# Sooner Pool forms, a three-step last map, group 0's first z tile moved, and another place for the third gate block

## The chip, the cores and the metric

The kernel runs on one core of one Trainium2 chip. The metric is the device time of one execution in microseconds (us). A core has engines that run side by side, each through its own list of instructions in order, and wait for one another by semaphores: PE (TensorE, the matmuls), ACT (ScalarE), DVE (VectorE), POOL (GpSimd) and SP (SyncE). SP, POOL and ACT also issue DMA transfers, each in the order of its own list.

## The reference

One layer of a hybrid trunk for 384 tokens (256 of a new stream, 8 times 16 of running ones), d_model 2048, in float32. One wide projection gives the columns for pool, z, x/B/C, dt and gates. Branch A is a causal pooling with a map for each of four channel groups; branch B is a Mamba-2 scan in eight groups; two gated projections are added, then an MLP follows.

```python
def pool_mixer(p, st, pos0, pool_w, pool_scale):
    ...
    for g, w in enumerate(POOL_WINDOWS):
        ...
        d = win / cnt[None, :, None] - p[:, :, lo:hi].astype(jnp.float32)
        outs.append(jnp.einsum('blc,cd->bld', d.astype(p.dtype), pool_w[g]))
    out = jnp.concatenate(outs, axis=-1) * pool_scale
    ...
        cb = jnp.einsum('btgn,bsgn->btsg', Cc, Bc)
        xdt = xc * dtc[..., None]
        y = jnp.einsum('btsgr,bsgrp->btgrp', cb[..., None] * decay, xdt)
        y = y + jnp.einsum('btgn,bgrpn->btgrp', Cc, h) * jnp.exp(cum)[..., None]
    ...
    br_pool = (a_pool @ p['w_pool_proj']).astype(jnp.float32)
    br_ssd = (a_ssd @ p['w_ssd_proj']).astype(jnp.float32)
    merged = (gates[:, :, 0] * br_pool + gates[:, :, 1] * br_ssd).astype(u.dtype)
    out = merged @ p['w_out']
```

## The kernel before

Weights come in units of 128 x 1024 floats, half a MB, that SP loads (`wfetch`, L64). Every float32 product is made of three: ACT copies a unit to a high half (`wh_...`, L71), DVE subtracts it for the low half (`wl_...`, L72), and PE multiplies high by high (L102), high by low (L103) and low by high (L104). A projected tile of 128 channels by 384 tokens uses two units, 24 matmuls each. `take` keeps up to three split units ahead, so that ACT makes one split for each 24 matmuls of PE, between other work. Both the loads on SP and the splits on ACT and DVE follow a queue of units that is written out (L988 on). A tile of a projection goes to one of two PSUM buffers (`mmtile`); what empties it runs on DVE.

PE's own order is forced: each `half` is issued behind the last matmul of the one before. A helper `behind(ins)` issues a piece after another, and `later()` puts it behind the newest weight split on ACT and on DVE. For the rest a scheduler sets each engine's order.

The Pool branch. Sixteen tiles p0 to p15 are projected, four for each of the maps 0 to 3 (`pool_tile`, L455 on: DVE empties the PSUM tile, L468 to L470, and ACT keeps the last rows, L478). `pool_map(gi)` multiplies the windowed tiles by the map's weights ("pw"), and ACT writes the scaled result to the tile px (L535). What follows is put on a list, `steps`: a `tick()` after each weight unit takes one entry of each list. The entries are five differences on DVE (`diff`), and five pieces, each a copy on ACT (L546), a subtraction on DVE (L547) and a store to DRAM (L548), from px to pf. Map 0 has four empty entries ahead of these. px and pf are single buffers, so that map 1 writes them only when map 0's pieces and stores are through. `dt_turn` (L615 on) turns the dt columns by 11 small PE transposes ("tk", L627) and copies them to `tok` on DVE (L628, L635); it stands behind tile (2, 1), which is p9.

The scan. Group 0 has its x, B, x, C, x, x tiles and four z tiles projected, in this order in the queue. A `conv_in` moves a tile to a cbuf with the last rows of the state; `taps` makes the convolution: a first tap on ACT (L678), three more on DVE (L680), a silu on ACT (L684, with a load of the activation table where another function ran before). `t_cb` multiplies C by B (cb, L753), `t_yi` multiplies the state hs by C (py, L762); then x's next tile is projected. Group 0's convolutions belong to the pool `phd`, whose first instruction comes behind the last of `phc`, with the pieces of map 3. `eside` (L894) and `expside` (L903) form the decay E on ACT. x is turned to tokens through DRAM (t_scr, L708 to L720, on POOL), and state comes by POOL too (hs, L741).

The end of the mixer's first half. Three blocks of the gate of branch A are stored to ga_scr for later (`stored`); the blocks 1 and 2 use the ring "hs" of the scan's pool for their output ("gat"). Block 2 (ga2, 24 matmuls for each of its eight weights) runs beside the end of the scan. Then the matrix products of w_pp and w_ssd begin, by a scheme of seven products from quarter blocks ("sq", L1229 to L1231). `load` (L1183 on) fetches four blocks b12, b11, b21, b22 on SP, and POOL adds b11's source to b12 by an accumulating DMA (L1189): that is U. W, V and b22 follow from it by sums on DVE (L1216). Slots of the left operand are read back from p_scr by `refill` (as, ab, aU, aW, aV, aX; L1303). "as" of the second block of rows is read at step 6 of the first.

The lines that touch all this in the code before:

Of the kernel before, what the change touches and what calls it, by code (L numbers as in the profile page):

```python
# [14 lines left out]
P = 128  # L15
# [18 lines left out]
def build(ctx, tc, io):  # L34
# [234 lines left out]
    def in_units(i):  # L269
        return [win[i - 5, 0], win[i - 5, 1]]  # L270
# [177 lines left out]
    with tc.tile_pool(name="phc", bufs=1, reuse_waits="tile") as pc, tc.tile_pool(name="phc2", bufs=2, reuse_waits="tile") as pc2:  # L448
# [73 lines left out]
        def pool_map(gi, after=None):  # L522
            for hf in range(2):
                h, l = wload(io["pool_w"][gi, hf], f"pw{gi}_{hf}")
                for n2 in range(2):
                    n = gi * 4 + hf * 2 + n2
                    o = sstile(f"pw{n}")[:, :T]
                    with behind(after):
                        for k in range(4):
                            c = slice((n2 * 4 + k) * P, (n2 * 4 + k + 1) * P)  # L530
                            mm3w(o, h[:, c], l[:, c], dd[gi][k][0], dd[gi][k][1], k == 0, k == 3)
                    if hf + n2 == 0:
                        x = pc.tile([P, 2, 10, P], F32, tag="px", name=f"px{gi}")
                    a = x[:, n2, hf * 3 : hf * 3 + 3].rearrange("p s t -> p (s t)")
# [14 lines left out]

            wait = [lambda: None] * (0 if gi else 4)  # L550
            steps.append(wait + [diff] + [lambda i=i: piece(i) for i in range(5)])

# [102 lines left out]
        for gi in range(4):  # L655
            for k4 in range(4):
# [9 lines left out]
                if gi == 1 and k4 > 1:  # L666
                    with later():
                        next(dt_steps, None)
                if (gi, k4) == (2, 1):
                    dt_turn()  # L670
# [3 lines left out]
    with tc.tile_pool(name="phd", bufs=2, reuse_waits="tile") as pd:  # L674
# [313 lines left out]
        for g in range(G):  # L988
            cs = [g * 4, 32 + g, g * 4 + 1, 40 + g, g * 4 + 2, g * 4 + 3]
            names = [f"x{c}" for c in cs] + [f"z{g}_{j}" for j in range(4)]  # L990
            queue.extend((in_units(17 + g * 10 + i)[q], f"{nm}_{q}") for i, nm in enumerate(names) for q in range(2))
        queue[:4] = []
        queue.extend(u for nb in (1, 2) for u in units_of("w_ga", nb))
        prev = None
        for g in range(G + 1):
            if g == G:
# [37 lines left out]

                stored("w_ga", 2, [mmtile("ga2_0"), sstile("ga2_1"), sstile("ga2_2")], gtiles(2), closing)
                break
# [40 lines left out]
            cside(D)  # L1077
            b2 = conv_in(u0 + 4, g * 4 + 2)
            S = D.p[0]
            S.py = mmtile(f"py{S.nm}")  # L1080
# [21 lines left out]

            def zproj(j):
                ps = proj(in_units(u0 + 6 + j), xg, f"z{g}_{j}")
                z = pd.tile([P, T], F32, tag="zs", name=f"zs{g}_{j}", bufs=8)
                with later():
                    v.tensor_tensor(halves(z), even_odd(ps), halves(rstd), ALU.mult)
                    s.activation(z, z, AF.Silu)
                D.zs.append(z)

            zproj(0)
            if g:
# [219 lines left out]
    def group(gk, np_):  # L1332
# [4 lines left out]
        def extra(i):  # L1337
# [25 lines left out]
            if gk < 3:  # L1363
                if t == 6:
                    refill(gk + 1, "s2")
                if t > 6:
                    refill(gk + 1, ORDER[t - 7])
                return
# [699 lines left out]
```

## Time and profile before

| | us |
|---|---|
| median of 3 runs | 2601.79 (2601.68 to 2604.74) |
| the profiled execution | 2603.8 |
| its span on the core | 2602.0 |
| PE busy in it | 2568.6 |
| ACT busy | 1697.5 |
| DVE busy | 2031.7 |
| POOL busy | 465.3 |

The span is the stretch of the core's own instructions; the profiled execution's time is 1.8 us longer. Times in a view are microseconds from the span's start. In a row of a timeline the first number is the start and the second the length; "x6" stands for six instructions that ran without a gap, and brackets hold the idle time of that engine before the row and what ended it. PE matmuls overlap: the distance of their starts is what one costs.

### The profile page before, as it was taken

The numbers are of one execution on the slowest core, as the hardware profiler recorded it, in microseconds if no ns is written. First come the engines' busy times: TensorE is split into PE (matmuls) and PEld (weight loads), VectorE is DVE, ScalarE is ACT, GpSimd is POOL, SyncE is SP. The second block draws the span as 40 slices with busy tenths as digits, with TensorE's granted clock in tenths as the row PEclk, the third lists the DMA queues.
The fourth block names the chain that finished last, engine by engine and source line by source line (L and its number), as shares of the span: only waits on it lengthen the run. The fifth ranks groups of instructions, "written<-read, shape, count | busy, mean of one in ns | idle before, by whom it ended". The sixth has DMA issues, their size and how long they took to land.

```text
span 2602.0 us, 40105 instructions
## 1 busy us (share of the span) xinstructions
PE 2568.6 (99%) x14953; PEld 2389.1 (92%) x14953; DVE 2031.7 (78%) x2843; ACT 1697.5 (65%) x2683; POOL 465.3 (18%) x695
## 2 busy tenths in 40 slices
PE   9998999999999999999999999999999999999998
PEld 8997999999999988888888888999999999999997
DVE  6786689999999875898888955767777777777778
ACT  6544657565756545877888644666666676767665
POOL 0011345445544512211111200000000000000000
PEclk9999999999999999999999999999999999999999
DMA  7566666676776658877666645555555555555554
GB/s 284 188 233 210 205 203 231 228 234 214 231 242 224 226 191 285 268 235 243 193 202 181 211 168 194 195 161 163 154 153 156 166 170 157 154 153 159 161 159 154
DMA packets 150098, 516.57 MB, mean 199 GB/s; under 512 B 22432, under 2 KB 25312, under 8 KB 144656
## 3 DMA queue, kind: packets, MB, share of 16 engines
q1 hardware_dynamic: 98944, 355.14, 40.8%
q0 software_dynamic: 43904, 144.07, 19.3%
q10 hardware_dynamic: 7056, 14.81, 1.8%
q8 instruction: 117, 1.92, 0.3%
q14 instruction: 77, 0.63, 0.1%
HBM read 453.57 MB, written 60.36 MB: 198 GB/s over the span
## 4 chain that ended last, share of the span: by engine, by line
PE 87%; DVE 5%; issue 4%; ACT 2%; DMA 2%; POOL 1%; SPq 0%; DVEq 0%; POOLq 0%; ACTq 0%
PE pj_up L102 6%; PE pj_up L103 6%; PE pj_up L104 6%; PE wd L1231 5%; PE wd L1230 5%; PE wd L1229 5%; PE pj_x L102 5%; PE pj_x L103 5%; PE pj_x L104 5%; PE pj_z L104 3%; PE sq L1230 3%; PE pj_z L102 3%; PE pj_z L103 3%; PE sq L1231 3%; PE sq L1229 3%
## 5 line engine op out<-in xcount | busy, mean ns | idle before, releaser
L71 ACT ACTIVATE wh_up<-w_up 128x1024 fp32r<-128x1024 f32 x126 | 133.1, 1057 | 219.0 <-PE pj_up L103 205.2
L102 PE MATMUL pj_x<-xgh,wh_x 128*128 128x384 f32 x768 | 252.5, 329 | 0.0
L103 PE MATMUL pj_x<-xgl,wh_x 128*128 128x384 f32 x768 | 250.8, 327 | 0.0
L104 PE MATMUL pj_x<-xgh,wl_x 128*128 128x384 f32 x768 | 250.8, 327 | 0.0
L102 PE MATMUL pj_up<-x1h,wh_up 128*128 128x384 f32 x768 | 250.5, 326 | 0.0
L103 PE MATMUL pj_up<-x1l,wh_up 128*128 128x384 f32 x768 | 250.4, 326 | 0.0
L104 PE MATMUL pj_up<-x1h,wl_up 128*128 128x384 f32 x768 | 250.4, 326 | 0.0
L72 DVE TENSOR_TENSOR wl_up<-w_up,wh_up 128x1024 fp32r<-128x1024 f32 x126 | 153.9, 1222 | 54.0 <-ACT wh_up L71 53.9
L1189 POOL DMA_DIRECT2D w_b_wd<-w_down x30 | 25.3, 843 | 832.9 <-DMA w_b_wd<-w_down 355.7
L104 PE MATMUL pj_z<-xgh,wl_z 128*128 128x384 f32 x512 | 167.0, 326 | 0.7 <-DVE wl_z L72 0.7
L102 PE MATMUL pj_z<-xgh,wh_z 128*128 128x384 f32 x512 | 167.0, 326 | 0.2 <-ACT wh_z L71 0.2
L103 PE MATMUL pj_z<-xgl,wh_z 128*128 128x384 f32 x512 | 166.9, 326 | 0.0
L102 PEld LDWEIGHTS pj_x<-xgh,wh_x 128*128 128x128 f32 x768 | 145.5, 189 | 2.5 <-issue 0.8
L103 PEld LDWEIGHTS pj_up<-x1l,wh_up 128*128 128x128 f32 x768 | 145.2, 189 | 1.2
L102 PEld LDWEIGHTS pj_up<-x1h,wh_up 128*128 128x128 f32 x768 | 145.2, 189 | 1.2
L103 PEld LDWEIGHTS pj_x<-xgl,wh_x 128*128 128x128 f32 x768 | 145.6, 190 | 0.0
L104 PEld LDWEIGHTS pj_x<-xgh,wl_x 128*128 128x128 f32 x768 | 145.4, 189 | 0.0
L104 PEld LDWEIGHTS pj_up<-x1h,wl_up 128*128 128x128 f32 x768 | 145.2, 189 | 0.0
L71 ACT ACTIVATE wh_x<-w_x 128x1024 fp32r<-128x1024 f32 x96 | 100.4, 1052 | 67.5 <-PE pj_x L103 30.5
L1206 ACT COPY acc<-wd 128x512 f32<-128x512 f32 x214 | 124.6, 582 | 23.8 <-PE wd L1231 23.8
L72 DVE TENSOR_TENSOR wl_x<-w_x,wh_x 128x1024 fp32r<-128x1024 f32 x96 | 116.7, 1219 | 25.8 <-ACT wh_x L71 25.8
L1229 PE MATMUL wd<-wh_b_wd,fh 128*128 128x512 f32 x360 | 136.4, 379 | 0.0
(495 smaller groups left out, 8193.9 us busy)
## 6 DMA issues: line engine op xcount, KB each, us to landing
w_up<-w_up SPq DMA_DIRECT2D x128, 512.0 KB, 4.1
w_b_wd<-w_down SPq DMA_DIRECT2D x120, 512.0 KB, 4.2
w_x<-w_in SPq DMA_DIRECT2D x96, 512.0 KB, 3.9
w_z<-w_in SPq DMA_DIRECT2D x64, 512.0 KB, 4.1
w_b_sq<-w_ssd SPq DMA_DIRECT2D x64, 512.0 KB, 5.1
w_ga<-w_ga SPq DMA_DIRECT2D x32, 512.0 KB, 3.6
hs<-ssm POOLq DMA_DIRECT2D x16, 1024.0 KB, 6.0
new_ssm_s<-hs POOLq DMA_DIRECT2D x16, 1024.0 KB, 4.3
```

The source lines that it names most:

```text
L71: cut[0] = s.activation(h, w, AF.Copy)
L72: cut[1] = v.tensor_tensor(l, w, h.bitcast(F32), ALU.subtract)
L102: te.matmul(out, wh, xh, start=first, stop=False, **how)
L103: te.matmul(out, wh, xl, start=False, stop=False, **how)
L104: return te.matmul(out, wl, xh, start=False, stop=last, **how)
L1189: summed[0] = gp.dma_start(w, unit(0, np_ * 2), accum_op=ALU.add)
L1206: s.copy(dst, o)
L1229: te.matmul(out, mh, vh, start=begin, stop=False, skip_group_check=held)
L1230: te.matmul(out, mh, vl, start=False, stop=False, skip_group_check=held)
L1231: te.matmul(out, ml, vh, start=False, stop=end, skip_group_check=held)
```

## The change

It has four parts.

- **Map 0's forms.** The list of map 0 has one empty entry ahead instead of four, and each map ticks once when its first product is made (L533 of the new file). `dt_turn` stands behind tile (2, 3), which is p11.
- **The last map in three steps.** Map 3's differences and five pieces are taken in three entries: differences and piece 0, pieces 1 and 2, pieces 3 and 4. The other maps keep six.
- **Group 0's first z tile.** In group 0 alone, z's first tile is projected ahead of cb and py, and its two units stand ahead of the last x tile's in the queue.
- **The third gate block.** ga2's three outputs go to tiles with the tags xT and cbc of the scan's pool, not to one tile of the ring hs. And "as" of the next block of rows is read behind the accumulating load of the block before (`summed[0]`).

```diff
@@ -530,6 +530,7 @@
                             c = slice((n2 * 4 + k) * P, (n2 * 4 + k + 1) * P)
                             mm3w(o, h[:, c], l[:, c], dd[gi][k][0], dd[gi][k][1], k == 0, k == 3)
                     if hf + n2 == 0:
+                        tick()
                         x = pc.tile([P, 2, 10, P], F32, tag="px", name=f"px{gi}")
                     a = x[:, n2, hf * 3 : hf * 3 + 3].rearrange("p s t -> p (s t)")
                     s.activation(halves(a), even_odd(o), AF.Copy, scale=vec[:, V_PSC + n : V_PSC + n + 1])
@@ -547,8 +548,12 @@
                     v.tensor_tensor(f[:, c, 1], src, f[:, c, 0].bitcast(F32), ALU.subtract)
                     gp.dma_start(p_scr[gi][:, c], f[:, c].rearrange("p s a k t -> p s (a k t)"))
 
-            wait = [lambda: None] * (0 if gi else 4)
-            steps.append(wait + [diff] + [lambda i=i: piece(i) for i in range(5)])
+            def several(*ns):
+                for n in ns:
+                    diff() if n < 0 else piece(n)
+
+            turns = ((-1, 0), (1, 2), (3, 4)) if gi == 3 else ((-1,), (0,), (1,), (2,), (3,), (4,))
+            steps.append([lambda: None] * (gi == 0) + [lambda ns=ns: several(*ns) for ns in turns])
 
         def dt_phase(pb):
             ps = mmtile("pj_dt")[:, :T]
@@ -666,7 +671,7 @@
                 if gi == 1 and k4 > 1:
                     with later():
                         next(dt_steps, None)
-                if (gi, k4) == (2, 1):
+                if (gi, k4) == (2, 3):
                     dt_turn()
         b0, b1 = conv_in(17, 0), conv_in(18, 32)
         pool_map(3, last[0])
@@ -987,8 +992,10 @@
         chain[0] = True
         for g in range(G):
             cs = [g * 4, 32 + g, g * 4 + 1, 40 + g, g * 4 + 2, g * 4 + 3]
-            names = [f"x{c}" for c in cs] + [f"z{g}_{j}" for j in range(4)]
-            queue.extend((in_units(17 + g * 10 + i)[q], f"{nm}_{q}") for i, nm in enumerate(names) for q in range(2))
+            names = [(i, f"x{c}") for i, c in enumerate(cs)] + [(6 + j, f"z{g}_{j}") for j in range(4)]
+            if not g:
+                names.insert(5, names.pop(6))
+            queue.extend((in_units(17 + g * 10 + i)[q], f"{nm}_{q}") for i, nm in names for q in range(2))
         queue[:4] = []
         queue.extend(u for nb in (1, 2) for u in units_of("w_ga", nb))
         prev = None
@@ -1032,7 +1039,11 @@
                     if len(count) == 6:
                         store(prev)
 
-                stored("w_ga", 2, [mmtile("ga2_0"), sstile("ga2_1"), sstile("ga2_2")], gtiles(2), closing)
+                tiles2 = [
+                    pd.tile([P, n, T], F32, tag=tag, name=f"gat2_{b}", bufs=bufs).rearrange("p a t -> p (a t)")[:, :512]
+                    for b, (n, tag, bufs) in enumerate(((2, "xT", 1), (2, "cbc", 2), (2, "cbc", 2)))
+                ]
+                stored("w_ga", 2, [mmtile("ga2_0"), sstile("ga2_1"), sstile("ga2_2")], tiles2, closing)
                 break
             u0 = 17 + g * 10
             D = Pair()
@@ -1076,6 +1087,17 @@
                 fside(prev.p[1], 1)
             cside(D)
             b2 = conv_in(u0 + 4, g * 4 + 2)
+
+            def zproj(j):
+                ps = proj(in_units(u0 + 6 + j), xg, f"z{g}_{j}")
+                z = pd.tile([P, T], F32, tag="zs", name=f"zs{g}_{j}", bufs=8)
+                with later():
+                    v.tensor_tensor(halves(z), even_odd(ps), halves(rstd), ALU.mult)
+                    s.activation(z, z, AF.Silu)
+                D.zs.append(z)
+
+            if not g:
+                zproj(0)
             S = D.p[0]
             S.py = mmtile(f"py{S.nm}")
             if g:
@@ -1100,15 +1122,8 @@
             with nullcontext() if g else behind(D.done):
                 eside(S, 0)
 
-            def zproj(j):
-                ps = proj(in_units(u0 + 6 + j), xg, f"z{g}_{j}")
-                z = pd.tile([P, T], F32, tag="zs", name=f"zs{g}_{j}", bufs=8)
-                with later():
-                    v.tensor_tensor(halves(z), even_odd(ps), halves(rstd), ALU.mult)
-                    s.activation(z, z, AF.Silu)
-                D.zs.append(z)
-
-            zproj(0)
+            if g:
+                zproj(0)
             if g:
                 with later():
                     prev.parts = norm_parts(pd, prev.ssum, f"g{prev.g}")
@@ -1362,7 +1377,8 @@
                 return
             if gk < 3:
                 if t == 6:
-                    refill(gk + 1, "s2")
+                    with behind(summed[0]):
+                        refill(gk + 1, "s2")
                 if t > 6:
                     refill(gk + 1, ORDER[t - 7])
                 return
```

What it does to the orders. A row has the line, the operation and "output<-inputs" with tile names; the number behind a name tells its buffers apart.

PE in the Pool phase, around the end of tile p10 (pj_p_1658 before, pj_p_1643 after) and the beginning of p11 (pj_p_1754, pj_p_1733) and p12 (pj_p_1844). Before:

```order
L104 MATMUL pj_p_1658<-xgh_522,wl_p_1_1698 128x384
L102 MATMUL pj_p_1754<-xgh_258,wh_p_0_1757 128x384
L103 MATMUL pj_p_1754<-xgl_259,wh_p_0_1757 128x384
L102 MATMUL pj_p_1844<-xgh_258,wh_p_0_1847 128x384
L103 MATMUL pj_p_1844<-xgl_259,wh_p_0_1847 128x384
L104 MATMUL pj_p_1754<-xgh_258,wl_p_0_1758 128x384
L102 MATMUL pj_p_1754<-xgh_279,wh_p_0_1757 128x384
```

And after:

```order
L104 MATMUL pj_p_1643<-xgh_522,wl_p_1_1680 128x384
L102 MATMUL pj_p_1733<-xgh_258,wh_p_0_1736 128x384
L103 MATMUL pj_p_1733<-xgl_259,wh_p_0_1736 128x384
L104 MATMUL pj_p_1733<-xgh_258,wl_p_0_1737 128x384
L102 MATMUL pj_p_1733<-xgh_279,wh_p_0_1736 128x384
```

The first two matmuls of p12 stood in the middle of p11; now p11 runs through. On DVE, the rows that end with the low half of p11 (wl_p_0_1758 before, wl_p_0_1737 after). Before, from the end of dt's turn on:

```order
L635 COPY tok<-tk_1637 64x64
L519 TENSOR_TENSOR dl_1634<-d_1628,dh_1633 128x384
L628 COPY tok<-tk_1653 128x192
L547 TENSOR_TENSOR pf_1538<-px_1488,pf_1538 128x2x256 x2
L468 TENSOR_TENSOR pbuf_678<-pj_p_1658,rstd 128x192
L469 TENSOR_TENSOR pbuf_678<-pj_p_1658,rstd 128x64
L470 TENSOR_TENSOR pbuf_678<-pj_p_1658,rstd 128x8x16
L72 TENSOR_TENSOR wl_p_0_1758<-w_p_0_1755,wh_p_0_1757 128x1024
```

And after:

```order
L468 TENSOR_TENSOR pbuf_680<-pj_p_1551,rstd 128x192
L469 TENSOR_TENSOR pbuf_680<-pj_p_1551,rstd 128x64
L470 TENSOR_TENSOR pbuf_680<-pj_p_1551,rstd 128x8x16
L499 TENSOR_TENSOR win_1_1628<-pbuf_680 128x518
L72 TENSOR_TENSOR wl_p_0_1737<-w_p_0_1734,wh_p_0_1736 128x1024
```

The low half of p11 came behind the emptying of p10; now it comes behind that of p9, one tile sooner, and no copy of dt's turn is near. ACT at the start of group 0's convolutions (pf of map 3, splits, first taps cacc, silus xs). Before:

```order
L71 ACTIVATE wh_x_0_2714<-w_x_0_2712 128x1024
L546 ACTIVATE pf_2479<-px_2429 128x2x256
L71 ACTIVATE wh_x_1_2751<-w_x_1_2749 128x1024
L546 ACTIVATE pf_2479<-px_2429 128x2x256
L71 ACTIVATE wh_z_0_0_2835<-w_z_0_0_2833 128x1024
L678 ACTIVATE cacc_2489<-cbuf_647,vec 128x384
L678 ACTIVATE cacc_2498<-cbuf_649,vec 128x384
```

And after, from the last pieces of map 3 on:

```order
L547 ACTIVATE pf_2479<-px_2429 128x2x256 x2
L71 ACTIVATE wh_x_1_2668<-w_x_1_2666 128x1024
L683 ACTIVATE cacc_2489<-cbuf_647,vec 128x384
L683 ACTIVATE cacc_2498<-cbuf_649,vec 128x384
L752 DMA cbc_0_0_2507<-cum_scr 128x768
```

And on ACT still after the change, from the first tap of C (cacc_2708) to C's silu:

```order
L683 ACTIVATE cacc_2708<-cbuf_647,vec 128x384
L71 ACTIVATE wh_z_0_0_2720<-w_z_0_0_2718 128x1024
L71 ACTIVATE wh_z_0_1_2754<-w_z_0_1_2752 128x1024
L443 COPY cbuf_649<-cstate 128x8x3
L71 ACTIVATE wh_x_0_2795<-w_x_0_2793 128x1024
L689 ACTIVATE xs_2616<-cacc_2611,vec 128x384
L689 ACTIVATE xs_2713<-cacc_2708,vec 128x384
```

The first taps move from behind the first split of z to behind the second split of group 0's third x tile. xs_2713, the silu of C that cb reads, stands behind three more splits. POOL at the third gate block (gat, ga_scr) and the reads from p_scr. Before:

```order
L220 DMA ga_scr_2_112<-gat_10951 128x512
L1303 DMA ab_11220<-p_scr_140 128x512
L1303 DMA as_11222<-p_scr_140 128x512
L1303 DMA ab_11224<-p_scr_140 128x2x512
L1303 DMA as_11458<-p_scr_141 128x512
L1189 DMA w_b_sq_0_11274<-w_pp 128x1024
L1303 DMA aU_11277<-p_scr_140 128x512
```

And after:

```order
L220 DMA ga_scr_2_112<-gat_2_10950 128x512
L1318 DMA ab_11222<-p_scr_140 128x512
L1318 DMA as_11224<-p_scr_140 128x512
L1318 DMA ab_11226<-p_scr_140 128x2x512
L1204 DMA w_b_sq_0_11276<-w_pp 128x1024
L1318 DMA aU_11279<-p_scr_140 128x512
L1318 DMA ab_11281<-p_scr_140 128x1024
L1318 DMA aW_11283<-p_scr_140 128x512
L1318 DMA aV_11285<-p_scr_140 128x512
L1318 DMA aX_11287<-p_scr_140 128x512
L1318 DMA as_11460<-p_scr_141 128x512
```

The second "as" (11458 before, 11460 after) moves from ahead of the accumulating load to behind aX.

## The prediction

> **What bounds the kernel now.** I read the page first, then TensorE's list of waits, then the timeline around each wait that is long, then the chain of work that ended last. The engine table and the wait list (columns: who waited for what, us in total, times, longest):
>
> ```profile
> PE 2568.6 (99%) x14953; PEld 2389.1 (92%) x14953; DVE 2031.7 (78%) x2843; ACT 1697.5 (65%) x2683; POOL 465.3 (18%) x695
> PE cb L753 <- ACT xs L684: 11.2, 1, 11.2
> PE sq L1230 <- DVE wl_b_sq L1177: 3.2, 3, 2.1
> PE pj_p L102 <- ACT pstg L478: 2.2, 1, 2.2
> ```
>
> PE is busy for 2568.6 of 2602.0 us, so a change that leaves the matmuls as they are can win only the 33 us in which PE is idle and the time that it runs slowly after an idle stretch. Three of the largest waits lie at the three places that this change touches. Everything else on PE keeps its work.
>
> **Place A, group 0's C.B product.** The timeline of PE (start, duration, and in brackets the idle time and its releaser), then that of ACT, then PE at the same step one group later:
>
> ```profile
> 243.12 0.33 PE L104 MATMUL pj_x<-xgh,wl_x 128*128 128x384 f32 x1
> 254.66 2.07 PE L753 MATMUL cb<-xs,xs 128*128 128x256 f32 x6 [11.21 <-ACT xs L684]
> 256.67 1.96 PE L762 MATMUL py<-hs,Cm 128*32 128x256 f32 x16
> 260.95 0.33 PE L103 MATMUL pj_x<-xgl,wh_x 128*128 128x384 f32 x1
> ...
> 240.38 0.61 ACT L546 ACTIVATE pf<-px 128x512 fp32r<-128x512 f32 x1
> 243.32 1.06 ACT L71 ACTIVATE wh_z<-w_z 128x1024 fp32r<-128x1024 f32 x1 [2.33 <-PE pj_x L103]
> 244.28 1.11 ACT L678 ACTIVATE cacc<-cbuf,vec 128x384 f32<-128x384 f32 x2
> 253.47 1.14 ACT L684 ACTIVATE xs<-cacc,vec 128x384 f32<-128x384 f32 x2 [2.25 <-DVE cacc L680]
> ...
> 344.14 1.04 PE L753 MATMUL cb<-xs,xs 128*128 128x256 f32 x6
> 345.02 0.38 PE L775 MATMUL Y<-cst,yis 128*128 128x128 f32 x2
> 346.81 1.09 PE L762 MATMUL py<-hs,Cm 128*32 128x256 f32 x16
> 347.83 0.72 PE L923 MATMUL su<-xd,Bd 32*128 32x256 f32 x16
> ```
>
> The convolution of group 0 begins on ACT only at 244.28, behind the last map's fifth piece (240.38) and the weight split at 243.32; cb waits for its silu. In group 1, cb takes 345.02 - 344.14 = 0.88 us and py 1.02; here, after 11.2 us of idling, they take about twice that, and so do the matmuls up to 260.95. The work between 243.28 (end of the row at 243.12, one matmul's 0.16 later) and 260.95 is 0.88 + 1.02 + seven projection matmuls of 0.162 (place C's spacing) = 3.0. **Lost at A: 17.67 - 3.04 = 14.6 us**, of which 11.2 are idle and 3.4 half speed.
>
> The change does two things here. The three-step map ends two weight splits after it begins, so the convolution moves up past the last three x splits. ACT does one split per 24 matmuls, 3.9 us, so it begins 11.7 us sooner; the silu of C, now behind the two z0 splits and one x split, ends about 245.5 instead of 254.6. And a z tile, 48 matmuls or 48 x 0.162 = 7.8 us, stands ahead of cb, which PE reaches at 243.3 + 7.8 = 251.1. The wait goes with 5.6 us to spare, and with it the half speed: **-14.6**. The z tile itself is only moved. What it needs, its two weights, takes the turns that x3 had; SP's loads are exchanged in the same way. The six accumulations on DVE (3.3 us) now stand ahead of z0's first low half, which I put at 243.4 where PE wants it at 243.8: hidden, by a margin of half a microsecond.
>
> What is late next is z3. ACT keeps E, its exponential and Bd in one row ahead of a weight split, which before cost this at z2's second half (PE, then ACT):
>
> ```profile
> 287.50 0.43 PE L102 MATMUL pj_z<-xgh,wh_z 128*128 128x384 f32 x1 [0.23 <-ACT wh_z L71]
> 288.76 0.43 PE L104 MATMUL pj_z<-xgh,wl_z 128*128 128x384 f32 x1 [0.67 <-DVE wl_z L72]
> ...
> 277.03 0.52 ACT L1108 ACTIVATE zs<-zs 128x384 f32<-128x384 f32 x1 [0.52 <-DVE zs L1107]
> 286.41 2.93 ACT L71 ACTIVATE wh_z<-w_z 128x1024 fp32r<-128x1024 f32 x3
> 289.36 1.28 ACT L1108 ACT_TABLE_LOAD   x1
> ```
>
> In the new order a table load (1.28) and one silu (0.52) come ahead of that split too. The new wait lies between 0 and 0.9 + 1.8 = 2.7; laid out by hand on ACT it comes to 1.7, of which 0.9 was there before: **+0.8**.
>
> **Place C, the early Pool maps.** PE, then DVE:
>
> ```profile
> 145.29 0.33 PE L103 MATMUL pj_p<-xgl,wh_p 128*128 128x384 f32 x1
> 147.79 0.40 PE L102 MATMUL pj_p<-xgh,wh_p 128*128 128x384 f32 x1 [2.18 <-ACT pstg L478]
> 148.83 0.69 PE L104 MATMUL pj_p<-xgh,wl_p 128*128 128x384 f32 x1 [0.47 <-DVE wl_p L72]
> 151.80 0.33 PE L104 MATMUL pj_p<-xgh,wl_p 128*128 128x384 f32 x1
> 153.42 0.33 PE L102 MATMUL pj_p<-xgh,wh_p 128*128 128x384 f32 x1
> ...
> 139.76 0.68 DVE L628 COPY tok<-tk 128x512 f32<-128x512 f32 x1
> 145.50 0.35 DVE L628 COPY tok<-tk 128x192 f32<-128x192 f32 x1
> 145.77 1.28 DVE L547 TENSOR_TENSOR pf<-px,pf 128x512 fp32r<-128x512 f32 x2
> 147.37 0.28 DVE L470 TENSOR_TENSOR pbuf<-pj_p,rstd 128x128 f32<-128x128 f32 x1
> ```
>
> The matmul at 147.79 is the first of tile 12, queued ahead of the rest of tile 11. It needs the PSUM buffer of tile 10, which DVE empties by 147.65, behind the tok copies and two pf pieces; the ACT copy that the list names is not what it must wait for. Normal spacing is (153.42 - 151.80)/10 = 0.162. From 145.45 to 151.80 stand 11 matmuls, 1.8 us of work. **Lost at C: 6.35 - 1.8 = 4.6 us.** After the change map 0's forms are done a tile sooner, map 1's are no longer held by them, and the turn of dt (11 small transposes on PE, eight copies on DVE that I put at 2.5 us in all: 0.68 and 0.35 above, and six of at most 0.3) comes two tiles later; tile 11's low half follows tile 10's evacuation, and PE runs the tiles in turn. I take the whole **-4.6**. At its new place the turn has tile 12's 7.8 us of matmuls over it: DVE does the copies and one tile's windows there, and the next map's low half is ready about 1 us before it is due. If that cover is gone it costs what is over, at most the 2.5.
>
> **Place B, the third gate block.** The chain that ended last (start, us, what); a row of POOL, one of SP and a window of PE (busy us, clock, DMA share, GB/s); then PE's spacing:
>
> ```profile
> 985.46 6.64 DMA ga_scr<-gat
> 994.51 13.72 DMA w_b_sq<-w_pp
> 1008.34 1.06 ACT wh_U_sq L1176
> ...
> 992.74 0.54 POOL L1303 DMA_DIRECT2D as<-p_scr  x1 [6.18 <-PE ga L157]
> 976.00 7.55 SPq L1186 DMA_DIRECT2D w_b_sq<-w_pp  x4
> 990.00:1000.00 10.00, 10.00 (x48) 1.00 1.07 409
> ...
> 1006.72 0.38 PE L1231 MATMUL sq<-wh_b_sq,ab 128*128 128x512 f32 x1
> 1008.67 0.38 PE L1231 MATMUL sq<-wh_b_sq,ab 128*128 128x512 f32 x1
> 1018.74 0.38 PE L1230 MATMUL sq<-wl_W_sq,aW 128*128 128x512 f32 x1
> ```
>
> The tile gat2 shares its ring with "as", so the load at 992.74 waits until gat2's last store lands (985.46 + 6.64), and the accumulating load of U stands behind it on POOL: issued 994.51, landed 1008.2, used 0.1 later. PE's spacing is 1.95/9 = 0.217; between 1008.89 and 1018.74 stand 19 matmuls, 4.1 us. **Lost at B: 9.85 - 4.1 = 5.7 us.** With gat2 in other memory that wait goes. U then waits for its own first load, which SP issues near 982.7 (it must now wait for the last z stores, whose memory it takes) and which lands near 989: issue about 989, landing by the old 13.7 us at 1003, where ACT needs it at 1007.8. **-5.7**, with 5 us to spare on U itself. The "as" of the next map goes behind U, out of its way. The other side: that first load, half a MB, now stands on SP right ahead of the gate weights that PE needs next. PE had no wait for them, so the new one lies between 0 and what half a MB takes: 1.3 us at the 409 GB/s of the window, 2.6 at half of that. I take **+0.8**, the 1.3 less some cover.
>
> **Sum:** -14.6 + 0.8 - 4.6 - 5.7 + 0.8 = -23.3. The profiled execution took 2603.8 (span 2602.0 and 1.8 around it), so 2580.5 by its own time; it lies 2.0 above the median 2601.8, so the forecast is **2578.5**.
>
> **The clock.** At C a wait of 2.18 and one of 0.47 were followed by half speed: 6.35 us less 2.65 of waiting is 3.7 for 11 matmuls that take 1.8. The Trainium skill, "TensorE: Matmul & The Clock Gate", Part 1, says that the array falls to half clock after at least one idle window of about 3.4 us, and advises no gaps above that. The trace disagrees at C, where 2.65 us in two waits were enough; by the page's rule my two new waits would cost only themselves.
>
> **The rivals.**
> (1) The new small waits pull the clock down, as at C, where the half speed cost 4.6 - 2.65 = 1.9. At both places that makes 2 x 1.9 = 3.8 more: 2582.3. For it: the rows of C; against it: the 0.9 at z2 pulled nothing down.
> (2) U stays late. The window shows the DMA engines full (share 1.07), so an earlier issue may only share the same bytes: B gains nothing and pays 0.8, so 2578.5 + 5.7 = 2584.2. Against it: "as" of the next map, 0.25 MB, is no longer ahead of U, and U's whole loss is made in the 4 us of splits and sums behind it, so 4 us sooner is enough.
> (3) The convolution does not come sooner, held by something other than its place in the row; then the z tile alone covers 7.8 of 11.2, and 3.4 of idling and 3.4 of half speed stay: 2585.3. Against it: nothing but the map's pieces stands ahead.
> (4) ACT and DVE bunch at z3 for 5 us instead of 1.7, with A's half speed behind it: 2578.5 + 3.3 + 3.4 = 2585.2. For it: nothing there is shorter than before, only sooner; against it: ACT's wait before E was for DVE, not for data.
> (5) Slower than before: the same two loads of state go out while weights are streaming, and not in PE's pause:
>
> ```profile
> hs<-ssm POOLq DMA_DIRECT2D x2, 1024.0 KB, 11.0
> ```
>
> Each took 11.0 us with PE paused, and x's turned copies stand behind them on POOL. If the pair's inputs came 2 x 11 us late, ACT's row would reach z3's split at 286.4 + 22 = 308.4, PE would be there at 251.1 + 1.9 + three tiles of 7.8 = 276.4: a wait of 32.0 in place of 1.7, with 3.4 of half speed, so 2578.5 + 33.7 = 2612.2. It passes the old time from 22 - 10.4 = 12 us of lateness on. Against it: with the convolution 11.7 us sooner the copies start sooner too, and no row of ACT ahead of that split waited for a DMA.
>
> **How the numbers follow.** Forecast 0.52 (2575 to 2580.5); (1) 0.15; (2) 0.12; (3) 0.06; (4) 0.06; little gained after all 0.04; (5) 0.05. The lower end is the sum without any new wait, 2601.8 - 24.9 - 0.9 = 2576, less a little: 2574.5. The upper end takes in (1) to (4) one at a time: 2588. About 0.2%, 5.2 us, is what a measurement of this kernel can tell from no change: faster 0.91, same 0.04, slower 0.05.
>
> **What would show it.** Right: no wait at cb over 0.5 us and a clock of 1.00 there; no PE wait between tiles 10 and 12; U landed before 1004 less the shift. Wrong: a wait over 3 us at z3 (4), a U that lands when PE is there (2), or a new large wait at the map that follows dt's turn.

## The result, and the profile after

| | before | after |
|---|---|---|
| median, us | 2602.05 (2601.68 to 2604.74, 4 runs) | 2585.03 (2584.42 to 2586.29, 4 runs) |
| ratio | | 0.9933, interval 0.9916 to 0.9950 |
| profiled execution and its span, us | 2603.8, 2602.0 | 2585.57, 2583.8 |

The kernel became 17.0 us faster by the medians. The forecast was 2578.5, 23.3 us less than before: the direction was right, the time lies in the range, and 6.3 us of the gain didn't come. To see where, I cut the execution at four marks that every kernel passes: the first gate matmul (near 54 us), the first product of map 2 (near 165), the first py of group 0's second pair (near 300) and the first matmul of the gate weight that runs inside w_pp's products (near 1029). Their starts come from PE's timeline. The three stretches between them hold the places C, A and B:

| kernel (profile) | C | A | B |
|---|---|---|---|
| before | 112.07 | 134.95 | 728.65 |
| after | 107.50 | 125.82 | 723.63 |
| change, us | -4.6 | -9.1 | -5.0 |
| forecast, us | -4.6 | -13.8 | -4.9 |

C and B came out as forecast to 0.1 us, and A brought 4.7 us less. That is closer than one profile of each can tell: kernels of the experiments whose edit leaves a stretch alone differ by 1.4 to 1.9 us in it (C 111.86 to 113.79, A 133.67 to 135.08, B 727.55 to 729.26). Further by the profile: the three changes sum to -18.7 and the spans differ by 18.2, mostly since the first mark itself came 0.8 later in this execution.

The list of PE's waits after the change:

```profile
PE pj_z L102 <- ACT wh_z L71: 2.9, 1, 2.9
PE gb L156 <- DVE wl_gb L72: 2.4, 7, 0.6
PE warm_o L291 <- DVE warm L287: 1.2, 1, 1.2
PE pj_x L102 <- DVE zs L1095: 0.9, 1, 0.9
PE sq L1245 <- DVE wl_b_sq L1192: 0.8, 2, 0.6
PE pj_z L104 <- DVE wl_z L72: 0.7, 1, 0.7
```

The 11.2 at cb is gone, as are the 2.2 in the Pool phase and the 2.1 behind U. At the top stands a wait that the list of before had at 0.2: the high half of a z unit. New is the x tile that waits for zs.

**Place C.** The same window before (us, PE busy and matmul rows, clock, DMA share, GB/s), which held the wait and the half speed:

```profile
140.00:160.00 20.00, 17.35 (x97) 0.91 0.71 243
```

and after:

```profile
140.00:160.00 20.00, 20.00 (x129) 1.00 0.60 197
```

**Place A.** PE after the change, from cb to the end of the slow stretch at z3:

```profile
247.29 1.04 PE L758 MATMUL cb<-xs,xs 128*128 128x256 f32 x6
248.26 1.09 PE L767 MATMUL py<-hs,Cm 128*32 128x256 f32 x16
250.21 0.43 PE L102 MATMUL pj_x<-xgh,wh_x 128*128 128x384 f32 x1 [0.86 <-DVE zs L1095]
...
276.79 0.43 PE L102 MATMUL pj_z<-xgh,wh_z 128*128 128x384 f32 x1 [2.91 <-ACT wh_z L71]
278.05 0.43 PE L104 MATMUL pj_z<-xgh,wl_z 128*128 128x384 f32 x1 [0.67 <-DVE wl_z L72]
278.80 0.50 PE L102 MATMUL pj_z<-xgh,wh_z 128*128 128x384 f32 x1
281.98 0.45 PE L103 MATMUL pj_z<-xgl,wh_z 128*128 128x384 f32 x1
```

cb starts with no wait and at full speed (1.04 for its six matmuls, 2.07 before). From 278.80 to 281.98 PE runs at half speed: ten matmuls in 3.2 us in place of 1.6. ACT and DVE over the same stretch:

```profile
240.93 1.06 ACT L71 ACTIVATE wh_x<-w_x 128x1024 fp32r<-128x1024 f32 x1 [3.53 <-DMA w_x<-w_in]
265.95 0.63 ACT L879 ACTIVATE xhl<-xT 128x512 fp32r<-128x512 f32 x1 [2.84 <-DVE xT L865]
267.60 2.43 ACT L899 ACTIVATE E<-cbc,tok 128x128 f32<-128x128 f32 x8
273.97 1.28 ACT L1096 ACT_TABLE_LOAD   x1
275.70 1.99 ACT L71 ACTIVATE wh_z<-w_z 128x1024 fp32r<-128x1024 f32 x2
...
249.64 0.52 DVE L1095 TENSOR_TENSOR zs<-pj_z,rstd 128x384 f32<-128x384 f32 x1
264.50 0.56 DVE L865 TENSOR_TENSOR xdt<-xT,tok 128x384 f32<-128x384 f32 x1 [2.80 <-DMA xT<-t_scr]
```

Two things are late that were not in the forecast. The weight of the last x tile lands only at 240.9, and ACT waits 3.5 us for it, with x's and C's silu queued behind. And x's turned copy comes back from DRAM 2.8 us after DVE wants it. ACT's row of E stands behind xhl, so the split of z3 comes at 275.70. Without the 2.84 that xhl waited it would begin at 272.86 and end at about 273.9, by my estimate, and PE is there at 273.7: the late copy accounts for nearly the whole wait of 2.91.

The chain of work that ended last (start, us, what) shows where the copy loses its time:

```profile
237.13 8.17 DMA t_scr<-xb
251.67 1.84 POOL t_scr L713 x3
253.52 5.71 DMA t_scr<-xb
261.05 3.42 DMA xT<-t_scr
267.69 2.34 ACT E L899 x8
```

A store of 48 KB of the first set took 8.17 us from issue to landing, where the median over the kernel is 4.0. From then to 251.67 POOL issued the fetches of B and of the first x, one after another; only then came the four stores of the second x, whose transpose DVE had ended at 246.0.

**Place B.** POOL, ACT and PE after the change:

```profile
974.80 0.99 POOL L1204 DMA_DIRECT2D w_b_sq<-w_pp  x1
992.09 1.06 ACT L1191 ACTIVATE wh_U_sq<-w_b_sq 128x1024 fp32r<-128x1024 f32 x1 [3.22 <-DMA w_b_sq<-w_pp]
984.27 0.48 PE L156 MATMUL ga<-wl_ga,xgh 128*128 128x512 f32 x1 [0.35 <-DVE wl_ga L72]
```

U's accumulating load was issued at 974.80. With the 13.0 us by which this part now runs sooner that is 988 in the times of before; the forecast said 989. It took 17.3 us until ACT could use it, not the 13.7 that I carried over, so U was there at 1005 in those times, 1 us after the 1004 that the prediction names as a sign, and still PE did not wait for it.

### The profile page after: what moved, and what is told of

The parts are those of the page before. It is cut to its first block, busy times and chain, and to the rows that moved or that the text cites. A ratio compares the mean times of both kernels' runs of the same rounds, so it can differ in the third digit from the quotient of the medians.

```text
span 2583.8 us, 40108 instructions
## 1 busy us (share of the span) xinstructions
PE 2564.7 (99%) x14953; PEld 2388.4 (92%) x14953; DVE 2031.9 (79%) x2843; ACT 1697.2 (66%) x2683; POOL 466.4 (18%) x695
## 4 chain that ended last, share of the span: by engine, by line
PE 84%; issue 7%; DVE 4%; DMA 2%; ACT 2%; POOL 1%; DVEq 0%; SPq 0%; POOLq 0%; ACTq 0%
PE pj_up L102 6%; PE pj_up L103 6%; PE pj_up L104 6%; PE wd L1245 6%; PE wd L1246 6%; PE wd L1244 6%; PE pj_x L102 4%; PE pj_x L103 4%; PE pj_x L104 4%; PE pj_z L104 3%; PE pj_z L102 3%; PE pj_z L103 3%; PE sq L1245 3%; PE sq L1246 3%; PE sq L1244 3%
## 5 line engine op out<-in xcount | busy, mean ns | idle before, releaser
L1245 PE MATMUL wd<-wl_b_wd,fh 128*128 128x512 f32 x360 | 136.4, 379 | 0.0
```

The costliest lines, as they stand in the source:

```text
L1245: te.matmul(out, mh, vl, start=False, stop=False, skip_group_check=held)
```

## The experiments

Each kernel ran beside the kernel before on the same chip. The stretches of the profile (C, A, B as above) tell the parts apart better than the whole time, which varies from run to run by 1.3 us in the steadiest of these kernels and by 9.6 in the least steady. Each kernel has one profile, so a stretch is one execution's, and differences of 1 to 2 us between two kernels in it are within the spread given above.

**The three parts alone.** The first: the tick, the one empty entry and the later turn.

```diff
                     if hf + n2 == 0:
+                        tick()
...
-            wait = [lambda: None] * (0 if gi else 4)
+            wait = [lambda: None] * (gi == 0)
...
-                if (gi, k4) == (2, 1):
+                if (gi, k4) == (2, 3):
```

> Only the first part of the change on the kernel before: map 0's forms begin sooner and dt's turn stands two tiles later. Theory: the whole loss of place C, 2.65 us of waiting and 1.9 of half speed, goes, and nothing comes in its place: 4.6 us less in the profile from tile p12 on, and 4 to 5 us less in the median (ratio about 0.998). Rival: the shift of about 4.6 that the changed kernel shows after this phase needs something of the other parts too; then this run gains under 2.5 us. Second rival: the earlier end of the phase is lost again at the C.B product of group 0, whose wait is made by ACT's order and moves with it: then the wait there grows above 11.2 us. The theory says 11.2 stays, since ACT's row moves with PE's.

Measured: 2596.83 against 2603.45, ratio 0.9977 (0.9968 to 0.9987). C takes 107.50, as in the changed kernel, and the wait at cb is still 11.2. The 6.6 us of the medians are more than the 4 to 5 expected; the place gives 4.6. The theory holds there; ACT's row moves with PE.

The second: the three entries of map 3 and the z move, with both of the change's hunks for them.

```diff
+            turns = ((-1, 0), (1, 2), (3, 4)) if gi == 3 else ((-1,), (0,), (1,), (2,), (3,), (4,))
...
+            if not g:
+                names.insert(5, names.pop(6))
...
+            if not g:
+                zproj(0)
```

> Only the second and third parts on the kernel before: the last map in three steps and group 0's first z tile ahead of cb. Theory: the wait at cb goes (14.6 us with its half speed), and 4 to 6 us come back behind it, in a wait of PE for the PSUM tile that zs empties (about 0.9), one for the high half of z3 (about 2.9), one for its low half (0.7) and about 1.8 of half speed; the median is 8.5 to 10.5 us below the kernel before (ratio about 0.9965). Rival: the returned time belongs to the first part of the change, which moved the phase against the DMA traffic; then this run gains 13 us or more and shows no wait over 1.5 at z3.

Measured: 2595.19, ratio 0.9978 (0.9969 to 0.9987). A takes 128.63, 6.3 less than before, and its waits are 3.4 at the x tile behind py and 1.5 and 0.7 at z3. So what came back is made by these two parts themselves, and the rival fell. It was more than the 4 to 6 expected: 14.6 less 6.3 is 8.3 by this profile. The profiled execution took 2598.49, 3.3 above the run's median, so the 6.3 may be too low.

The third: the other memory and the order of "as".

```diff
-                stored("w_ga", 2, [mmtile("ga2_0"), sstile("ga2_1"), sstile("ga2_2")], gtiles(2), closing)
+                tiles2 = [
...
+                stored("w_ga", 2, [mmtile("ga2_0"), sstile("ga2_1"), sstile("ga2_2")], tiles2, closing)
...
-                    refill(gk + 1, "s2")
+                    with behind(summed[0]):
+                        refill(gk + 1, "s2")
```

> Only the fourth part on the kernel before: the third gate block in the tiles of tags xT and cbc, and the next block's as read behind the accumulating load. Theory: the three waits around U and the half speed behind them go (5.7 us), a wait of 0.3 to 1 us for a gate weight comes in: 4.5 to 5.4 us less. The accumulating load is issued about 12 us after the last z store instead of about 16, and lands 17 us later because the DMA engines are full. Rival: the gain in the changed kernel came from the new times of everything ahead, not from this edit; then U still lands late here and under 2 us are gained.

Measured: 2598.30, ratio 0.9980 (0.9971 to 0.9989); B takes 724.23, 4.4 less. It stands by itself. The three parts' medians differ from the kernel before by 6.6, 8.3 and 5.2 us, 20.0 in all against the 17.0 of the whole change; the product of the three ratios, 0.9935, is near its 0.9933, and their stretches sum to 15.3 against 18.7. So the parts add up only roughly.

**Which half of A does it.** The z move alone:

```diff
+            if not g:
+                names.insert(5, names.pop(6))
...
+            if not g:
+                zproj(0)
```

> Only the z tile of group 0 ahead of cb, on the kernel before; the last map keeps its six entries. Theory: the convolution begins where it began, behind the first split of the third x tile's successor, so that the silu of C still ends near 254.6 us (plus what tile C's phase moves); PE reaches cb 7.8 us later, and the wait at cb falls from 11.2 to about 3.4, with half speed behind it that costs 2 to 3.5: the phase ends 4 to 8 us sooner than before, less what comes back at z3. Rival: the z tile alone is enough (wait at cb under 1).

One run, 2597.43; A takes 128.20, 6.7 less. cb no longer waits, which was the rival's sign, but for a reason that the expectation did not have. PE, and DVE:

```profile
249.49 0.66 PE L102 MATMUL pj_z<-xgh,wh_z 128*128 128x384 f32 x1 [6.04 <-ACT xs L684]
...
248.73 1.14 DVE L436 TENSOR_TENSOR cbuf<-pj_x,rstd 128x192 f32<-128x192 f32 x4
```

The z tile waits itself, 6.0 us. There are two PSUM buffers for projected tiles, and z's is that of C's tile, which DVE empties only at 248.73, behind the six first accumulations of the convolution. In the program the matmul waits for that instruction; the silu which the list names merely ended next to it.

The three entries alone:

```diff
+            turns = ((-1, 0), (1, 2), (3, 4)) if gi == 3 else ((-1,), (0,), (1,), (2,), (3,), (4,))
```

> Only the last map in three entries, on the kernel before; cb keeps its place behind the x tile. Theory: the silu of C stands behind one split of z on ACT and ends about 2.3 us after PE has reached cb: the wait at cb falls from 11.2 to 2 to 3, with up to 2 of half speed: 9 to 12 us sooner at cb, some of it lost again at z2 or z3. Rival: the DMA engines are then full with weights and state, the weight of z0 lands late as that of x3 did in the changed kernel, and holds ACT's row: then the wait at cb is 4 to 6.

One run, 2593.28; A takes 124.98, 10.0 less. This half alone brings at least as much as both together (9.1 in the changed kernel, 6.3 in the run with these two parts). PE:

```profile
246.43 1.14 PE L757 MATMUL cb<-xs,xs 128*128 128x256 f32 x6 [2.57 <-ACT xs L688]
```

The wait is the 2 to 3 us expected. So the z move was tried as the only thing to leave out:

```diff
-            if not g:
-                names.insert(5, names.pop(6))
...
-            if not g:
-                zproj(0)
```

> The changed kernel without the z move: first, second and fourth part only, cb in its old place. Theory: the three-step map alone brings 10.2 us of the place (run with the three steps only), more than both together (9.1), because x's third tile comes ahead of z in the queue again and its weight, its silu and the turned copies are not held up; the sum is 4.6 + 10.2 + 4.9 = 19.7, so 2 to 3 us less than the changed kernel, about 2582 to 2583, with a wait of about 2.6 at cb and 0.9 at z2. Rival: with the first part in, the phase moves against the loads and the z move is needed; then the wait at cb is over 5 us and the time at or above that of the changed kernel.

Measured: 2584.85, ratio 0.9931 (0.9918 to 0.9945): the time of the changed kernel, not 2 to 3 us less. A takes 124.90 (125.82 with the z move). The wait at cb is 2.2, and py runs at half speed behind it. The rival fell too: the z move is not needed. It exchanges a wait at cb for waits at the x tile and z3, of about the same size.

**What comes back at A.** First, less load in the full stretch:

```diff
-                gp.dma_start(o[:, 0], scr[:P])
+                pooled[0] = gp.dma_start(o[:, 0], scr[:P])
...
-            pload(D.p[1])
+            with nullcontext() if g else behind(pooled[0]):
+                pload(D.p[1])
```

> The changed kernel, with one more edit: in group 0 the load of the second pair's state (1 MB, hs_1) stands on POOL behind the fetches of x's turned tiles and no longer right behind the first pair's. Theory A: what came back at z3 is made by the DMA engines being full from 228 to 243 us: a weight of the last x tile lands 3.5 us late and holds up ACT's row with x's silu in it, so x's turned copy is 2.8 us late on DVE, and E with it. With 1 MB less in that stretch (2.4 us at 425 GB/s) the weight lands 1.5 to 3 us sooner, ACT's wait for it falls to 0.5 to 2, DVE's wait for xT to under 1.5, and PE's wait at z3 from 2.9 to about 1, too short for half speed: 3 to 5 us less than the changed kernel. Theory B: the wait at z3 is ACT's own queue (E, its exponential, the table load and the silu of z ahead of the split); then it stays above 2.5 and the time is that of the changed kernel within 1 us. A third outcome is that the later load itself is waited for by the second pair: then a new wait shows at its py or its scaling on DVE, near 285 us.

Measured: 2584.30, ratio 0.9930 (0.9918 to 0.9942). A takes 126.32, no better, in an execution that took 2587.15, 2.9 above the run's median. ACT, then PE:

```profile
240.22 1.06 ACT L71 ACTIVATE wh_x<-w_x 128x1024 fp32r<-128x1024 f32 x1 [2.86 <-DMA w_x<-w_in]
263.81 0.63 ACT L881 ACTIVATE xhl<-xT 128x512 fp32r<-128x512 f32 x1 [4.28 <-DMA t_scr<-xb]
...
249.50 0.43 PE L102 MATMUL pj_x<-xgh,wh_x 128*128 128x384 f32 x1 [0.16 <-DVE zs L1097]
272.73 0.69 PE L102 MATMUL pj_z<-xgh,wh_z 128*128 128x384 f32 x1 [3.46 <-ACT wh_z L71]
```

The weight lands only 0.7 us sooner, not 1.5 to 3. The wait at the x tile does go (0.86 to 0.16). But in the compiled order E's row now stands ahead of z2's second split instead of z3's, so it meets PE one unit sooner, and the wait is 3.5 there. By its letter theory B holds (the wait stays above 2.5, and the time is within 1 us). But with the order changed the run doesn't decide between A and B as it was meant to; it shows that the place of E's row on ACT counts.

Then E itself, which needs none of the turned x:

```diff
-            with nullcontext() if g else behind(S.split):
+            with nullcontext() if g else behind(cut[0]):
                 eside(S, 1)
                 expside(S)
```

> The changed kernel, with one edit: in group 0 the second half of E and E's exponential stand on ACT behind the newest weight split and no longer behind the split of x's turned copy (xhl). They need only cbc and tok. Theory B, revised: PE's wait at z3 is ACT's row, which runs E, a table load, the exponential and another table load in one piece behind xhl, and xhl waits 2.8 us for x's turned copy; with E's part done before xhl, in idle time of ACT, the split of z3 is ready in time: the waits 2.9 and 0.7 and the half speed of 1.8 behind them go, 4.5 to 5.5 us less than the changed kernel, about 2580. The 0.9 at the tile that zs empties stays. Theory A, that the late copy holds PE by itself, through another path than E's place: then a wait over 1.5 us stays at z2 or z3.

Measured: 2581.64, ratio 0.9925 (0.9912 to 0.9937). The waits at z2 and z3 are under 0.3 in all, as theory B says, but that does not yet show it: the wait at the x tile grew to 2.5 with half speed behind it, so that PE comes to z2 and z3 3.3 us later, counted from the first product of map 2. A takes 123.31, 2.5 less than after the change, not 4.5 to 5.5. PE, then DVE, then rows with z3's first split on ACT (the second of two) and its first low half on DVE (the first of two):

```profile
251.20 0.43 PE L102 MATMUL pj_x<-xgh,wh_x 128*128 128x384 f32 x1 [2.46 <-DVE zs L1095]
...
246.64 0.58 DVE L708 STREAM_TRANSPOSE xb<-xs 128x384 f32<-128x384 f32 x1 [2.89 <-DMA t_scr<-xb]
...
267.50 2.18 ACT L71 ACTIVATE wh_z<-w_z 128x1024 fp32r<-128x1024 f32 x2
...
274.67 2.35 DVE L72 TENSOR_TENSOR wl_z<-w_z,wh_z 128x1024 fp32r<-128x1024 f32 x2
```

PE begins z3 at 276.38. Its first split is ready at 269.7, in time even for a PE 3.3 us sooner: E's row no longer holds it. Its first low half is ready at 275.9, behind a DVE that waited 2.2 us for xT; a PE 3.3 us sooner would, by these times, have waited some 2.5 us for that.

DVE works in order: ahead of zs, which empties z's PSUM tile, stands the transpose of x into xb, and xb is free only when its last store to t_scr has landed. So another buffer for z:

```diff
+                bank[0] = sstile
                 zproj(0)
+                bank[0] = mmtile
```

> The kernel of the run with E's part freed, and in addition group 0's first z tile in one of the six other PSUM buffers, so that the next x tile needn't wait until zs is through. Theory: the wait of 0.9 at that x tile goes as well: 0.5 to 1 us less than that run (2579 or so). Rival: the six buffers are short there, and cb or a later product waits instead, by as much.

Measured: 2584.33, ratio 0.9929 (0.9916 to 0.9943). The wait at the x tile is gone and its like stands further on. DVE, then PE:

```profile
264.16 0.56 DVE L865 TENSOR_TENSOR xdt<-xT,tok 128x384 f32<-128x384 f32 x1 [3.06 <-DMA xT<-t_scr]
...
268.47 0.54 PE L104 MATMUL pj_z<-xgh,wl_z 128*128 128x384 f32 x1 [2.95 <-DVE wl_z L72]
```

A low half of z2 stands on DVE behind xdt, which waits 3.1 us for the turned copy. So with E freed and PE in time the wait is still there, one tile sooner. Last, both edits that took a wait away, on the changed kernel: the two diffs above of the later state and of E's place.

> The changed kernel with both edits: E's second part and its exponential freed from xhl, and the second pair's state loaded behind the fetches of x's turned tiles. Theory: two things are late in group 0, the x tile's weight and the turned copies of x (each store to t_scr waits in a full DMA stretch, and DVE, in order, waits for xb's buffer and for xT). With 1 MB less ahead, DVE's wait for xb goes, so the wait of PE at the x tile after py is under 0.3 (it was 2.5 with E freed alone); with E freed, the wait at z2 and z3 is under 1.5 in all. Sum about 5 us under the changed kernel: 2579 to 2581. Rival: DVE still waits 2 to 3 us for xT ahead of a low half of z2; then a wait of 2 to 3.5 at z2 stays with half speed behind it and the time is that of the run with E freed, 2581 to 2584.

Measured: 2583.98, ratio 0.9927 (0.9915 to 0.9940); A takes 123.59. No wait at the x tile, and at z2:

```profile
267.24 0.43 PE L102 MATMUL pj_z<-xgh,wh_z 128*128 128x384 f32 x1 [1.61 <-ACT wh_z L71]
268.50 0.43 PE L104 MATMUL pj_z<-xgh,wl_z 128*128 128x384 f32 x1 [0.67 <-DVE wl_z L72]
```

with DVE still waiting 2.2 us for xT, and half speed from 269.60 to 272.80. The rival holds. So E's place decides where PE waits; freeing it did not take the wait away in any run in which PE was in time. All of these kernels are within 3.4 us of the changed one, and their intervals overlap with its: none is shown to beat it, though the one with E freed has the lowest median and its five runs (2580.29 to 2583.97) lie below all four of the changed kernel.

**The halves of C and B.** Two kernels with one half of each, read by place; one run each.

```diff
-                if (gi, k4) == (2, 1):
+                if (gi, k4) == (2, 3):
...
+                tiles2 = [
```

> Two halves of parts, at places 850 us apart, read by place: of the first part only the later turn of dt (map 0's forms begin where they began), of the fourth only the other memory for the third gate block (the read of the next block's as stays ahead of the accumulating load). Theory: at the Pool tiles the turn's eight copies on DVE were what held up the emptying of p10, so the wait goes and 3.5 to 4.6 us are gained there; at the end of the mixer the waits around U go nearly whole, since the memory was what the loads waited for: 4 to 5.5 us. Rivals: the pieces of map 0 were the cause at the Pool tiles (gain under 1.5); the order behind the accumulating load was half of it (gain under 3 at U).

Measured: C takes 108.20, 3.9 less: the later turn of dt is enough but for a wait of 0.4. B takes 725.57, 3.1 less, with U used at 1003.76 after an issue at 985.10 and a wait of 1.9 left behind it: just above the rival's 3.

```diff
+                        tick()
...
+            wait = [lambda: None] * (gi == 0)
...
+                    with behind(summed[0]):
+                        refill(gk + 1, "s2")
```

> The other halves: map 0's forms begin sooner, dt's turn stays; the next block's as is read behind the accumulating load, the third gate block stays in the ring hs. Theory: the order alone gains at most 1 us at U, since its load still waits for the gate block's store; at the Pool tiles PE's order is mended by this half as well (p12's start stands behind p11 in the compiled order), so that it gains 2 to 4.6 us there too, and the two halves don't add. Rival: with the turn in its old place its copies still hold up the emptying, and the wait of 2 us stays.

Measured: C takes 107.51, the whole 4.6, with the turn where it was. So either half ends the wait at p12, and the two don't add. B takes 726.80, 1.9 less, where 1 us at most was expected; POOL's wait stays:

```profile
986.64 0.54 POOL L1304 DMA_DIRECT2D as<-p_scr  x1 [6.28 <-PE ga L157]
```

In five kernels that leave B as it was, it took 727.55 to 729.26, so the 3.1 and 1.9 say little. PE's waits around U say more: 3.3 us in the kernel before, 3.1 with the order alone, 1.9 with the memory alone, 0.7 with both (the third part's run). And the 1.9 of the order alone is mostly half speed: behind a wait of 2.09 the kernel before runs eight matmuls slowly, which costs about 1.7 us. This run has the same wait and no slow matmuls, and neither have three of the kernels that leave B as it was. So by the waits both halves are needed, from one profile of each kernel.

## Why the prediction was right, and where it was off

- **What bounds the kernel** was read rightly: only PE's waits, with the half speed behind them, were to be had, and the gain is made at the three places named.
- **Place C, -4.6:** right in size and place. As a cause I named the late forms and the turn together; mending either one alone is nearly enough (4.6 and 3.9, one run each).
- **Place B, -5.7 and +0.8:** right in the cause, and nearer in size than it deserved. The two terms measured -5.0 together. The new wait for the gate weight was 0.35, inside its bounds of 0 to 2.6, so that U brought about 5.4. Of the 5.7 some 1.7 is half speed in the kernel before, which four other kernels with the same wait did not have. That U would land in the old 13.7 us was wrong (17.3), but the margin of 5 us covered it.
- **Place A, -14.6:** the wait at cb and its half speed went, as said. The reason that I gave for the z tile's part was wrong: it does not cover 7.8 us whatever else happens. With the old start of the convolution it waits 6.0 us itself, for the PSUM buffer of C's tile; rival (3) was worked out with this error. The three-step map alone brings A's whole gain (10.0); the z tile alone brings 6.7, and adds nothing to it.
- **The term that failed is "+0.8" at z3.** It measured 2.9 + 0.7 of waiting and 1.7 of half speed, 5.3 in place of the 0.9 of before: +4.4. The waiting alone, 3.6, is above the bound of 2.7 that I gave it. The sum by hand on ACT took x's turned copy to be there when wanted; it came 2.8 us late, and E's row, with a table load and an exponential that need no x, stood behind it. A second wait had no term: 1.0 at the x tile behind py (0.86 of waiting and a slow first matmul), whose PSUM buffer zs frees. -14.6 + 4.4 + 1.0 = -9.2, against 9.1 measured.
- **Rivals.** (4) is what happened in kind, with the half speed of (1). That its time, 2585.2, is the 2585.0 measured is luck: it put 6.7 us on the forecast, and the place came out 4.7 above it; most of the rest is the 2.0 taken off to come to the median, while the profile after lies only 0.5 above its own. Its argument against, that ACT's row waited for DVE and not for data, was drawn from a trace in which PE stood still for 11 us and the copies had that time to land. (5) has the right beginning, loads of state that meet the weight stream, and far too high a price.

The cause behind both late things was not settled by a run. The DMA engines are full there: this window of the changed kernel shows share and GB/s in its last columns.

```profile
230.00:240.00 10.00, 10.00 (x64) 1.00 1.05 399
```

The Trainium skill, "DMA: Bandwidth & Descriptors", section "Issuing engines are not separate DMA queues", says that transfers from any engine run on the same 16 DMA engines and interleave. The trace agrees: between 225 and 250 us the state loads took 12.2 us each in the median and the x weights 8.4, against 6.2 and 3.8 over the whole kernel. But POOL's order has its part, as the chain above shows: the second x's stores stand behind the fetches of B and of the first x, 5.7 us after its transpose. Taking 1 MB away moved the weight by 0.7 us only, and DVE's wait for the copy from 2.8 to 2.0. Loads of state from another queue, or x's stores ahead of B's fetches without another change of ACT's order, were not tried.

## What to carry to other kernels

A wait taken from PE moves everything behind it forward, but not the transfers that had used the pause: look in the trace of before at what ran on DMA while PE stood still, and give each of those a due time of its own. When a piece of work is put in front of a wait to cover it, see first that its own buffers are free at that time. And a group of instructions that an in-order engine runs as one row should not stand behind a load that only its neighbour needs.

## What the runs showed of the hardware

Half speed came after shorter waits of PE than I had thought, and the same wait did not always bring it. Read by the spacing of the matmuls, there was none after 0.86 us, after 0.67 twice within 1.3 us (the first part alone) or after a single 1.94 (the run of turn and tiles). After a single 2.16 (the kernel without the z move), cb and py ran at half speed at once. Ahead of the slow stretch of 3.6 us in the kernel with E freed stood one wait of 2.46, and full speed went on for four matmuls first. Two waits did it as well: 1.54 with 0.67 (the two parts of group 0) and 1.61 with 0.67 (both edits), neither of them over 2 us.

At U six kernels have the same two waits of PE at the same distance, 0.78 and then 2.09. In two of them, the kernel before and that with the three entries alone, half speed followed; in the other four it did not. So the length of the wait does not decide alone.

Mostly it cost 1.6 to 2.3 us. But it was 3.1 after 3.46 (the later state), 3.4 after 11.2 at cb in the kernel before, and about 3.5 after 2.58 at place C in the third part's run. The Trainium skill, "TensorE: Matmul & The Clock Gate", Part 1, puts the gap at about 3.4 us; in these runs 2.1 to 2.2 was enough, though not always, so that any wait or pair of waits of PE over 2 us is better priced at its length and about 2 us more, with an uncertainty of as much.
